# A hybrid decoder trunk on one core: gate and up of 2048 FFN columns by seven products of halves

## The chip, the cores and the metric

The kernel runs on one core of one Trainium2 chip. The metric is the device time of one execution in microseconds (us); of several runs the median is given. The profile is one execution recorded by the hardware profiler.

## What is computed

Two layers over 256 tokens of width 1024, in fp32. Layer 0 mixes tokens by gated linear attention, layer 1 by causal softmax attention with partial rotary positions. Each mixer and each feed-forward layer (FFN) is followed by a residual and a layer norm. The change touches the FFN alone:

```python
FFN_HIDDEN = 2816
def swiglu_ffn(x, w_gu, w_down):                     # x (256, 1024), w_gu (1024, 5632), w_down (2816, 1024)
    gate, up = jnp.split(x @ w_gu, 2, axis=-1)
    return (jax.nn.silu(gate) * up) @ w_down
# x <- LN(alpha*x + mixer(x));  x <- LN(alpha*x + swiglu_ffn(x))
```

## The kernel before

Every operation is entered in a plan (`Plan.op`) with its engine, an estimated length, and the tiles it reads and writes. `emit()` then places each engine's operations in time by these lengths, greedily: what can start first goes first, among equals the one that stands earlier in the program, with some operations marked urgent. The resulting order on each engine is fixed; at run time each engine works through its own list and waits by semaphores. Buffers of 4 KB per partition (kind S, 38 slots) are handed out in program order: a new buffer is given out only when enough slots stay free for all earlier buffers that have none yet. So loads, which stand on SP's queue, run ahead of their use as far as the slots allow. PSUM has four banks of kind acc, which hold the sums of the down product for the whole FFN, and four of kind ps.

Weights are fp32. A unit of 512 KB (128 partitions x 1024) is loaded by SP and split by `split`: ACT copies it into a rounded high part (L258), DVE subtracts that from the raw unit to give the low part (L259). `w_kcols` takes slices of the contraction, `w_row` one row block of the down weights. A product is three matmuls (`mm3`, L286 to L288): high by high, low by high, high by low. The activations are kept transposed and split as well (tiles xT, kind T); `transpose_split` makes them by four 128x128 transposes on PE into one PSUM bank (L301), a copy on ACT (L310) and a subtraction on DVE (L314).

In `ffn` the first 512 of the 2816 columns are computed with tokens in rows: stationary xT, moving weights of 512 columns (banks pg and pu, `act_block`), silu on ACT (L439), the product on DVE (L440), then `transpose_split` into hT0. The other 2304 columns are nine rounds of 256 columns with features in rows: stationary weights of 128 columns, moving xT of both token halves, 256 wide (bank gu), so that silu (L480), product (L482) and split (L485, L487) leave hT already in the layout that the down product needs. Each round needs four units (g and u, two slices each). A row block of 128 of these columns is then multiplied by its row of the down weights (`down`, banks fy, 512 wide, both token halves); the list `pend` delays it by a round, and the last three rounds' (six row blocks) come at the end, one half of the output at a time, each token half followed by its `layer_norm`. In the layer norm GpSimd (POOL) takes a power of one column (L354); POOL has next to nothing else to do in the FFN.

Of the kernel before, what the change touches and what calls it, by code (L numbers as in the profile page):

```python
# [11 lines left out]
AF = mybir.ActivationFunctionType  # L12
# [4 lines left out]
P = 128  # L17
# [17 lines left out]
SLOTS = 38  # L35
# [5 lines left out]
class Buf:  # L41
    """A tile of the plan: gets a slot of its kind when its first writer is placed."""
# [147 lines left out]
def kernel(ctx, tc, x, positions, gla_w_in, gla_w_gk, gla_b_gk, gla_norm_g, gla_w_out,  # L190
# [104 lines left out]
    def transpose_split(src, dst, t, half, skey=None, dstf=None, dkey=None, n=4):  # L295
# [38 lines left out]
    def layer_norm(xo, y, gb, dstT, t, last=False):  # L334
# [21 lines left out]
        for hf in range(2):  # L356
# [13 lines left out]
            else:  # L370
                transpose_split(xn, dstT, t, hf, skey=hf)
        return xn

# [37 lines left out]
    def out_proj(aT, w, xo, gb, dstT):  # L411
        ws = [w_row(f"wo{k}", w, k) for k in range(KT)]
        xn = []
        for t in range(2):
# [8 lines left out]
            xn.append(layer_norm(xo[t], y, gb, dstT, t))  # L423
        return xn

# [1 line left out]
    def ffn(i, xs, T, gb, dstT, last):  # L427
# [31 lines left out]
        NB = (HID - 512) // 256  # L459
        for b in range(NB):  # L460
# [297 lines left out]
    xs = out_proj(ogT, gla_w_out[0], xs, gb, T1)  # L758

# [41 lines left out]
    xs = ffn(0, xs, T1, gb, T2, False)  # L801

# [113 lines left out]
    xs = out_proj(oT, moba_w_out[0], xs, gb, T3)  # L916
    gb = load_ln(1, 1)
    ffn(1, xs, T3, gb, None, True)
# [39 lines left out]
```

## Time and profile before

| | us |
|---|---|
| median of 3 runs | 608.55 (606.66 to 609.45) |
| span of the profiled execution | 605.5 |
| PE busy | 592.4 (98%) |
| DVE busy | 385.4 (64%) |
| ACT busy | 282.7 (47%) |
| POOL busy | 23.4 (4%) |
| DMA queue q1, share of 16 engines | 55.4% |

The profiled execution has no time beside its span; the runs' median lies 3.05 us above it. In the 40 slices PE is at 9 tenths in all but the first and the last. Matmul durations of single rows overlap, since matmuls are pipelined; the distance from one start to the next is what one costs.

### The profile page before, as it was taken

Reading aid. Unit: us, or ns where it says so; the run is one execution under the profiler, and the core shown is the slowest. Engines: PE = TensorE matmul, PEld = TensorE weight load, DVE = VectorE, ACT = ScalarE, POOL = GpSimd, SP = SyncE. Lnnn points to the kernel's source line nnn. Section 1 sums busy time; section 2 is a strip of 40 time slices with the busy share of each in tenths; the row PEclk is TensorE's granted clock in tenths of the full one; section 3 lists DMA queues with packets and bytes.
Section 4 is the critical chain, followed back from the end, with each engine's and each line's share of the span. In section 5 each row is a group of like instructions: output and inputs, shape, how many; then the busy total and the mean of one; then the engine's idle time right before and its main releaser. Section 6 shows DMA issues by size and latency. Waiting matters only on the chain.

```text
span 605.5 us, 9405 instructions
## 1 busy us (share of the span) xinstructions
PE 592.4 (98%) x3806; PEld 538.3 (89%) x3806; DVE 385.4 (64%) x523; ACT 282.7 (47%) x396; POOL 23.4 (4%) x27
## 2 busy tenths in 40 slices
PE   7999999999999999999999999999999999999995
PEld 6899887888899999999889999888899999999983
DVE  5897269986554555454695788999665554555226
ACT  4892365355444344444363456637454444444110
POOL 1020211100000000000000000000000000000001
PEclk9999999999999999999999999999999999999998
DMA  8974194667655556545375455536765665665001
GB/s 280 381 223 159 63 296 159 211 203 227 195 186 190 178 175 209 178 171 175 104 244 180 146 164 193 188 110 239 246 207 176 207 197 186 193 184 180 2 2 69
DMA packets 68270, 110.13 MB, mean 182 GB/s; under 512 B 4689, under 2 KB 42097, under 8 KB 68226
## 3 DMA queue, kind: packets, MB, share of 16 engines
q1 hardware_dynamic: 68226, 109.53, 55.4%
q8 instruction: 30, 0.49, 0.3%
q14 instruction: 14, 0.11, 0.1%
HBM read 108.47 MB, written 1.05 MB: 181 GB/s over the span
## 4 chain that ended last, share of the span: by engine, by line
PE 94%; DMA 3%; DVE 1%; ACT 0%; issue 0%; POOL 0%; SPq 0%; DVEq 0%; ACTq 0%
PE gu L286 11%; PE gu L288 11%; PE gu L287 11%; PE fy L286 7%; PE fy L288 7%; PE fy L287 7%; PE v L288 2%; PE v L286 2%; PE v L287 2%; PE y L286 2%; PE y L288 2%; PE y L287 2%; PE tr L301 1%; PE mq L286 1%; PE mk L288 1%; PE mk L286 1%
## 5 line engine op out<-in xcount | busy, mean ns | idle before, releaser
L482 DVE TENSOR_TENSOR sil<-gu,sil 128x256 f32<-128x256 f32 x36 | 15.3, 424 | 53.0 <-ACT sil L480 53.0
L480 ACT ACTIVATE sil<-gu 128x256 f32<-128x256 f32 x36 | 13.8, 384 | 63.9 <-PE gu L288 63.9
L354 POOL TENSOR_TENSOR st<-st,mhalf 128x1 f32<-128x1 f32 x8 | 7.6, 944 | 496.8 <-DVE st L352 496.8
L487 DVE TENSOR_TENSOR hT<-sil,hT 128x256 fp32r<-128x256 f32 x36 | 15.2, 424 | 13.7 <-ACT hT L485 13.7
L485 ACT CAST hT<-sil 128x256 fp32r<-128x256 f32 x36 | 14.6, 406 | 17.3 <-DVE sil L482 17.3
L310 ACT CAST xT<-tr 128x512 fp32r<-128x512 f32 x16 | 8.7, 588 | 22.4 <-PE tr L301 22.4
L314 DVE TENSOR_TENSOR xT<-tr,xT 128x512 fp32r<-128x512 f32 x16 | 10.4, 685 | 5.7 <-ACT xT L310 5.6
L342 DVE SCALAR_TENSOR_TENSOR r<-xn,fy 128x512 f32<-128x512 f32 x8 | 5.5, 684 | 11.3 <-PE fy L288 11.3
L346 DVE BATCH_NORM_STATS2 st<-r 128x6 f32<-128x512 f32 x16 | 11.1, 694 | 0.5
L364 DVE SCALAR_TENSOR_TENSOR xn<-r,st,lnb 128x512 f32<-128x512 f32 x16 | 11.3, 744 | 0.0
L360 DVE SCALAR_TENSOR_TENSOR r<-r,st,lng 128x512 f32<-128x512 f32 x16 | 11.2, 744 | 0.0
L734 DVE SCALAR_TENSOR_TENSOR og<-o,ss,sg 128x256 f32<-128x256 f32 x8 | 3.5, 476 | 5.9 <-POOL sg L695 5.9
L695 POOL TENSOR_TENSOR sg<-sg,normg 128x512 f32<-128x512 f32 x4 | 6.4, 1594 | 15.1 <-ACT sg L691 15.1
L866 ACT ACTIVATE pr<-ms,mst 128x128 f32<-128x128 f32 (+1 forms) x16 | 6.6, 422 | 0.6 <-DVE mst L861 0.6
L301 PEld LDWEIGHTS tr<-ident,xn 128*128 128x128 f32 x48 | 5.6, 141 | 0.8
L301 PE MATMUL tr<-ident,xn 128*128 128x128 f32 x48 | 6.2, 272 | 0.0
L310 ACT CAST hT0h<-tr 128x512 fp32r<-128x512 f32 x4 | 2.3, 585 | 7.1 <-PE tr L301 7.1
L691 ACT ACTIVATE sg<-g 128x512 f32<-128x512 f32 x4 | 2.4, 594 | 6.9 <-PE g L288 6.8
L517 PE MATMUL junk<-zeros 128*128 128x128 f32 x22 | 4.4, 375 | 1.1 <-DVE zeros L510 1.1
L834 DVE TENSOR_TENSOR sw<-sw,rope 32x512 f32<-32x512 f32 x8 | 5.4, 672 | 0.0
L751 DVE TENSOR_TENSOR ogT<-trg,ogT 128x512 fp32r<-128x512 f32 x4 | 2.7, 682 | 4.1 <-ACT ogT L747 4.1
L259 DVE TENSOR_TENSOR u10l<-u10r,u10h 128x1024 fp32r<-128x1024 f32 x2 | 2.5, 1226 | 4.5 <-ACT u10h L258 4.5
(1207 smaller groups left out, 2439.0 us busy)
## 6 DMA issues: line engine op xcount, KB each, us to landing
lng<-in_ln_g SPq DMA_DIRECT2D x4, 512.0 KB, 4.0
lnb<-in_ln_b SPq DMA_DIRECT2D x4, 512.0 KB, 6.3
x<-in_x SPq DMA_DIRECT2D x4, 256.0 KB, 4.2
g00r<-in_ffn_w_gu SPq DMA_DIRECT2D x2, 512.0 KB, 3.5
g01r<-in_ffn_w_gu SPq DMA_DIRECT2D x2, 512.0 KB, 4.5
u00r<-in_ffn_w_gu SPq DMA_DIRECT2D x2, 512.0 KB, 7.0
u01r<-in_ffn_w_gu SPq DMA_DIRECT2D x2, 512.0 KB, 8.1
d0r<-in_ffn_w_down SPq DMA_DIRECT2D x2, 512.0 KB, 7.4
```

The source lines that it names most:

```text
L286: nc.tensor.matmul(ps, lh, rh, start=start, stop=False)
L287: nc.tensor.matmul(ps, ll, rh, start=False, stop=False)
L288: nc.tensor.matmul(ps, lh, rl, start=False, stop=stop)
L301: nc.tensor.transpose(ps.f[:, j * P:(j + 1) * P], src.f[:, k * P:(k + 1) * P], ident.f)
L310: nc.scalar.copy(view(0), ps.f.rearrange("p (k c) -> p k c", k=4))
L346: nc.vector.bn_stats(st.f[:, 6 * hf:6 * hf + 6], r.f[:, sl])
L360: nc.vector.scalar_tensor_tensor(out=r.f[:, sl], in0=r.f[:, sl], scalar=st.f[:, 12:13], in1=g.f[:, sl], op0=ALU.subtract, op1=ALU.mult)
L364: nc.vector.scalar_tensor_tensor(out=xn.f[:, sl], in0=r.f[:, sl], scalar=st.f[:, 15:16], in1=b.f[:, sl], op0=ALU.mult, op1=ALU.add)
L480: act(256, lambda ps=ps, sil=sil: nc.scalar.activation(sil.f[:, 0:S], ps.f[:, 0:S], AF.Silu), [ps], [(sil, 0)], table="silu")
L482: dve(256, lambda ps=ps, sil=sil: nc.vector.tensor_tensor(out=sil.f[:, S:2 * S], in0=ps.f[:, S:2 * S], in1=sil.f[:, 0:S], op=ALU.mult), [p ...
L485: act(256, lambda c=c, sil=sil, hT=hT: nc.scalar.copy(hv(hT)[:, c, :], sil.f[:, S:2 * S]), [(sil, 1)], [(hT, c)])
L487: dve(256, lambda c=c, sil=sil, hT=hT: nc.vector.tensor_tensor(out=hv(hT)[:, 2 + c, :], in0=sil.f[:, S:2 * S], in1=hv(hT)[:, c, :].bitcast ...
```

## The change

For four blocks of 512 columns (the columns 512 to 2559) of each layer, gate and up are computed together as a product of 2x2 block matrices: the left matrix has the two token halves as rows and the two halves of the contraction as columns, the right one the two halves of the contraction as rows and gate and up as columns. Seven products of halves, with sums of x on the left and sums of weights on the right, take the place of eight. Tokens stand in rows: stationary parts of x, moving weights of 512 columns.

The sums of x (s1 to s4) are made once a layer by `x_sums` from an unsplit copy of the transposed x, which `transpose_split` now keeps (`keep`, an added ACT copy), and are split like everything else. The sums of weights are made in place: a unit is loaded by SP and split for its product, and then an accumulating DMA on POOL's queue (`dma_add`) adds the next quarter of the weights into the same buffer, which is split again. The chain `ch` goes through four products (a00, s1, s2, a11) with three such adds; `r4` goes through two (s4, s3) with one; `r3` is used once (a01). All seven products collect in three PSUM banks (pa, pc, pb), evicted in between by `keep_`. The results stand with tokens in rows, so each token half is transposed and split once a block. The down products of the block before are placed between the products (`down_now`). The last 256 columns stay as they were, and SLOTS is 41.

```diff
-SLOTS = 38
+SLOTS = 41
...
+    def dma_add(fn, reads, writes, **kw):
+        return pl.op("POOL", 1.3, fn, reads, writes, extra=4.0, **kw)
...
@@ transpose_split
             act(512, hi, [ps], [(dst, ("h",) + kh)], urgent=True)
             dve(512, lo, [ps, (dst, ("h",) + kh)], [(dst, ("l",) + kh)], urgent=True)
+            if keep is not None:
+                act(512, lambda: nc.scalar.copy(keep[t].f[:, 512 * half:512 * half + 512], ps.f), [ps],
+                    [(keep[t], half)], urgent=True)
...
+    def x_sums(x32):
...
+        s13, s24 = S_("s13"), S_("s24")
+        out_ = {}
+        parts = (("s1", s13, 0, lambda: half(1, 0), lambda: half(1, 1), ALU.subtract, [(x32[1], 0), (x32[1], 1)]),
+                 ("s2", s24, 0, lambda: s13.f[:, 0:512], lambda: half(0, 0), ALU.subtract, [(s13, 0), (x32[0], 0)]),
+                 ("s3", s13, 1, lambda: half(0, 0), lambda: half(1, 0), ALU.subtract, [(x32[0], 0), (x32[1], 0)]),
+                 ("s4", s24, 1, lambda: half(0, 1), lambda: s24.f[:, 0:512], ALU.add, [(x32[0], 1), (s24, 0)]))
+        for n, b, j, a0, a1, op, reads in parts:
...
+            dve(512, lambda b=b, sl=sl, a0=a0, a1=a1, op=op: nc.vector.tensor_tensor(
+                out=b.f[:, sl], in0=a0(), in1=a1(), op=op), reads, [(b, j)])
+            hl = S_(n + "hl", True)
+            act(512, lambda b=b, sl=sl, hl=hl: nc.scalar.copy(hl.r[:, 0:512], b.f[:, sl]), [(b, j)], [(hl, 0)])
+            dve(512, lambda b=b, sl=sl, hl=hl: nc.vector.tensor_tensor(
+                out=hl.r[:, 512:1024], in0=b.f[:, sl], in1=hl.f[:, 0:512], op=ALU.subtract), [(b, j), (hl, 0)],
+                [(hl, 1)])
...
+        def unit(kh, gu, q, c0):
+            k0 = 4 * kh + 2 * q
+            return wgu[k0 * P:(k0 + 2) * P, HID * gu + c0:HID * gu + c0 + 512].rearrange("(k p) c -> p k c", p=P)
...
+        def split_unit(name, raw):
+            hi, lo = S_(name + "h", True), S_(name + "l", True)
+            act(1024, lambda: nc.scalar.copy(hi.r, raw.f), [raw], [hi])
+            dve(1024, lambda: nc.vector.tensor_tensor(out=lo.r, in0=raw.f, in1=hi.f, op=ALU.subtract), [raw, hi], [lo])
+            return hi, lo
...
+        def seven(b, c0, pend):
+            pa, pc, pb = pl.buf("ps", "pa"), pl.buf("ps", "pc"), pl.buf("ps", "pb")
+            e1, e2 = S_("e1"), S_("e2")
...
+            def product(ps, left, ws, first, last_):
+                st, rd = lhs(left)
+                for q, (wh, wl) in enumerate(ws):
+                    def f(q=q, wh=wh, wl=wl):
+                        for j in range(2):
+                            sh, sl_ = st(2 * q + j)
+                            cs = slice(512 * j, 512 * j + 512)
...
+                    pe(6 * 512, f, rd + [wh, wl], [ps])
...
+            def add_to(raws, kh, gu):
+                for q in range(2):
+                    def f(q=q):
+                        nc.gpsimd.dma_start(uv(raws[q]), unit(kh, gu, q, c0), accum_op=ALU.add)
+                    dma_add(f, [raws[q]], [raws[q]])
+
+            ch = [load_unit(f"A{q}", unit(0, 0, q, c0)) for q in range(2)]
+            product(pa, "a00", [split_unit(f"A{q}", ch[q]) for q in range(2)], True, False)
+            keep_(pa, e1, 0)
+            add_to(ch, 0, 1)
+            product(pc, "s1", [split_unit(f"B{q}", ch[q]) for q in range(2)], True, False)
+            keep_(pc, e2, 0)
+            r3 = [load_unit(f"C{q}", unit(1, 0, q, c0)) for q in range(2)]
+            product(pb, "a01", [split_unit(f"C{q}", r3[q]) for q in range(2)], True, True)
...
+            add_to(ch, 1, 1)
+            product(pa, "s2", [split_unit(f"D{q}", ch[q]) for q in range(2)], False, False)
+            keep_(pa, e1, 1)
+            r4 = [load_unit(f"E{q}", unit(1, 1, q, c0)) for q in range(2)]
+            down_now(pend[:2])
+            product(pc, "s4", [split_unit(f"E{q}", r4[q]) for q in range(2)], False, True)
...
+            transpose_split(e1, (h, l), 0, 0, skey=0, dkey=0, dstf=lambda i: dst(i, slice(0, P)))
+            add_to(r4, 0, 1)
+            product(pa, "s3", [split_unit(f"F{q}", r4[q]) for q in range(2)], False, False)
...
+            down_now(pend[2:])
+            add_to(ch, 1, 0)
+            product(pa, "a11", [split_unit(f"G{q}", ch[q]) for q in range(2)], False, True)
...
+            transpose_split(e2, (h, l), 1, 1, skey=1, dkey=1, dstf=lambda i: dst(i, slice(P, 2 * P)))
...
-        NB = (HID - 512) // 256
-        for b in range(NB):
+        for b in range(4):
+            pend = seven(b, 512 + 512 * b, pend)
+        for b in (8,):
             c0 = 512 + 256 * b
...
-            if b < NB - 2:
-                for k, bufs, f in pend:
-                    ws = w_row(f"d{k}", wd, k)
-                    for t in range(2):
-                        down(k, t, bufs, f, ws)
-                pend = []
```

## Rows read from the trace of the kernel before

**Rows 1.** The page, parts 1 and 2: busy time, and tenths in 40 slices
```profile
PE 592.4 (98%) x3806; PEld 538.3 (89%) x3806; DVE 385.4 (64%) x523; ACT 282.7 (47%) x396; POOL 23.4 (4%) x27
...
PEclk9999999999999999999999999999999999999998
DMA  8974194667655556545375455536765665665001
```

**Rows 2.** The page, part 4: the chain that ended last, share by engine
```profile
PE 94%; DMA 3%; DVE 1%; ACT 0%; issue 0%; POOL 0%; SPq 0%; DVEq 0%; ACTq 0%
```

**Rows 3.** Busy time by stretch: length, each engine's busy us, clock, DMA share, GB/s
```profile
core 0: us, PE busy (x) PEld busy (x) DVE busy (x) ACT busy (x) POOL busy (x), PEclk, DMA share, GB/s
...
90.00:120.00 30.00, 28.81 (x133) 23.11 (x132) 27.91 (x51) 13.54 (x17) 3.36 (x3) 1.00 0.56 184
120.00:150.00 30.00, 28.67 (x164) 24.97 (x163) 22.13 (x24) 15.93 (x19) 0.71 (x1) 1.00 0.67 221
...
201.00:218.00 17.00, 17.00 (x123) 16.04 (x122) 8.96 (x10) 6.82 (x10) 0.00 (x0) 1.00 0.57 186
```

**Rows 4.** The chain in order of time, 411 to 424: start us, us held, what
```profile
411.94 0.24 PE pg L286
...
417.31 0.23 PE pg L288
417.55 0.87 PE tr L301 x8
```

**Rows 5.** PE in order of time, 185 to 196: start, duration, operation (pipelined)
```profile
184.88 0.28 PE L288 MATMUL gu<-xT,u20h 128*128 128x256 f32 x1
...
193.64 0.40 PE L286 MATMUL fy<-d6h,hT 128*128 128x512 f32 x1
...
195.93 0.39 PE L287 MATMUL fy<-d6h,hT 128*128 128x512 f32 x1
```

**Rows 6.** One unit of the fifth round: ns min/median/max, first and last start
```profile
L256 SPq DMA_DIRECT2D g50r<-in_ffn_w_gu x2: 378/378/379, 193.8 to 486.5; - x2
L258 ACT CAST g50h<-g50r x2: 1051/1052/1052, 197.8 to 491.4; 128x1024 fp32r<-128x1024 f32 x2
L259 DVE TENSOR_TENSOR g50l<-g50r,g50h x2: 1226/1226/1226, 198.9 to 492.5; 128x1024 fp32r<-128x1024 f32 x2
...
DMA to landing us min/median/max: 3.9/4.4/4.8
...
L286 PE MATMUL gu<-xT,g50h x16: 277/281/283, 233.1 to 529.2; 128*128 128x256 f32 x16
```

**Rows 7.** Lines L439, L440, L310 and L314: ns min/median/max, first and last start
```profile
L439 ACT ACTIVATE sil<-pg x4: 584/597/611, 125.6 to 430.1; 128x512 f32<-128x512 f32 x4
...
L440 DVE TENSOR_TENSOR sil<-pu,sil x4: 680/683/683, 129.8 to 435.8; 128x512 f32<-128x512 f32 x4
...
L310 ACT CAST xT<-tr x16: 576/588/594, 5.1 to 418.5; 128x512 fp32r<-128x512 f32 x16
...
L314 DVE TENSOR_TENSOR xT<-tr,xT x16: 679/683/692, 5.7 to 419.3; 128x512 fp32r<-128x512 f32 x16
```

**Rows 8.** DMA of the stretch 15 to 30: packets, rate, share of 16 engines
```profile
DMA packets 3398, 5.71 MB, mean 381 GB/s; under 512 B 360, under 2 KB 744, under 8 KB 3397
...
q1 hardware_dynamic: 3397, 5.70, 105.4%
```

**Rows 9.** DMA issues of the stretch 105 to 125: KB each, us to landing
```profile
fu02r<-in_ffn_w_gu SPq DMA_DIRECT2D x1, 512.0 KB, 3.4
...
u01r<-in_ffn_w_gu SPq DMA_DIRECT2D x1, 512.0 KB, 8.1
```

**Rows 10.** The first unit behind the opening 512 columns: issue and first use
```profile
L256 SPq DMA_DIRECT2D g00r<-in_ffn_w_gu x2: 367/368/368, 113.6 to 407.2; - x2
...
L286 PE MATMUL gu<-xT,g00h x16: 277/282/365, 140.8 to 439.8; 128*128 128x256 f32 x16
```

**Rows 11.** Waits of SP's queue: us in total, times, longest
```profile
SPq L256 <- PE gu L288: 62.8, 23, 5.4
```

**Rows 12.** The page, part 5: POOL's part of the layer norm
```profile
L354 POOL TENSOR_TENSOR st<-st,mhalf 128x1 f32<-128x1 f32 x8 | 7.6, 944 | 496.8 <-DVE st L352 496.8
```

More of the change, by code (lines that the diff above doesn't have):

```diff
@@ L293, in new_T, with transpose_split @@
         return b
-    def transpose_split(src, dst, t, half, skey=None, dstf=None, dkey=None, n=4):
+    def transpose_split(src, dst, t, half, skey=None, dstf=None, dkey=None, n=4, keep=None):
         ps = pl.buf("ps", "tr")
@@ L332, in load_ln, with layer_norm @@
         return g, b
-    def layer_norm(xo, y, gb, dstT, t, last=False):
+    def layer_norm(xo, y, gb, dstT, t, last=False, keep=None):
         g, b = gb
@@ L370, in layer_norm @@
             else:
-                transpose_split(xn, dstT, t, hf, skey=hf)
+                transpose_split(xn, dstT, t, hf, skey=hf, keep=keep)
         return xn
@@ L422, in out_proj, with half, ffn @@
                 pe(3 * 512, f, aT.keys(t, k) + list(ws[k]), [y[hf]])
-            xn.append(layer_norm(xo[t], y, gb, dstT, t))
+            xn.append(layer_norm(xo[t], y, gb, dstT, t, keep=keep))
         return xn
-    def ffn(i, xs, T, gb, dstT, last):
+    def x_sums(x32):
+        def half(t, kh):
+            return x32[t].f[:, 512 * kh:512 * kh + 512]
+        s13, s24 = S_("s13"), S_("s24")
[5 more added lines that the diff above has]
+        for n, b, j, a0, a1, op, reads in parts:
+            sl = slice(512 * j, 512 * j + 512)
+            dve(512, lambda b=b, sl=sl, a0=a0, a1=a1, op=op: nc.vector.tensor_tensor(
[5 more added lines that the diff above has]
+                [(hl, 1)])
+            out_[n] = hl
+        return out_
+    def ffn(i, xs, T, gb, dstT, last, x32):
         wgu, wd = ffn_w_gu[i], ffn_w_down[i]
@@ new lines, in down_now, with keep_, dst @@
+        def down_now(items):
+            for k, bufs, f in items:
+                ws = w_row(f"d{k}", wd, k)
+                for t in range(2):
+                    down(k, t, bufs, f, ws)
+        def seven(b, c0, pend):
[8 more added lines that the diff above has]
+                            cs = slice(512 * j, 512 * j + 512)
+                            nc.tensor.matmul(ps.f, sh, wh.r[:, cs], start=first and q == 0 and j == 0, stop=False,
+                                             skip_group_check=True)
+                            nc.tensor.matmul(ps.f, sl_, wh.r[:, cs], start=False, stop=False, skip_group_check=True)
+                            nc.tensor.matmul(ps.f, sh, wl.r[:, cs], start=False, stop=last_ and q == 1 and j == 1,
+                                             skip_group_check=True)
+                    pe(6 * 512, f, rd + [wh, wl], [ps])
+            def keep_(ps, dst, j):
+                sl = slice(512 * j, 512 * j + 512)
+                act(512, lambda: nc.scalar.copy(dst.f[:, sl], ps.f), [ps], [(dst, j)])
+            def add_to(raws, kh, gu):
[11 more added lines that the diff above has]
+            product(pb, "a01", [split_unit(f"C{q}", r3[q]) for q in range(2)], True, True)
+            dve(512, lambda: nc.vector.tensor_tensor(out=e1.f[:, 0:512], in0=pb.f, in1=e1.f[:, 0:512], op=ALU.add),
+                [pb, (e1, 0)], [(e1, 0)])
+            act(512, lambda: nc.scalar.activation(e1.f[:, 0:512], e1.f[:, 0:512], AF.Silu), [(e1, 0)], [(e1, 0)],
+                table="silu")
+            add_to(ch, 1, 1)
[4 more added lines that the diff above has]
+            product(pc, "s4", [split_unit(f"E{q}", r4[q]) for q in range(2)], False, True)
+            h, l = S_(f"hT{b}h", True), S_(f"hT{b}l", True)
+            def dst(i, cs):
+                return (h, l)[i].r.rearrange("p (k c) -> p k c", k=4)[:, :, cs]
+            dve(512, lambda: nc.vector.tensor_tensor(out=e1.f[:, 512:1024], in0=pc.f, in1=e1.f[:, 512:1024],
+                                                     op=ALU.subtract), [pc, (e1, 1)], [(e1, 1)])
+            dve(512, lambda: nc.vector.tensor_tensor(out=e1.f[:, 0:512], in0=e1.f[:, 0:512], in1=e1.f[:, 512:1024],
+                                                     op=ALU.mult), [(e1, 0), (e1, 1)], [(e1, 0)])
+            transpose_split(e1, (h, l), 0, 0, skey=0, dkey=0, dstf=lambda i: dst(i, slice(0, P)))
+            add_to(r4, 0, 1)
+            product(pa, "s3", [split_unit(f"F{q}", r4[q]) for q in range(2)], False, False)
+            dve(512, lambda: nc.vector.tensor_tensor(out=e2.f[:, 0:512], in0=e2.f[:, 0:512], in1=pa.f,
+                                                     op=ALU.subtract), [pa, (e2, 0)], [(e2, 0)])
+            down_now(pend[2:])
+            add_to(ch, 1, 0)
+            product(pa, "a11", [split_unit(f"G{q}", ch[q]) for q in range(2)], False, True)
+            act(512, lambda: nc.scalar.activation(e2.f[:, 512:1024], pa.f, AF.Silu), [pa], [(e2, 1)], table="silu")
+            dve(512, lambda: nc.vector.tensor_tensor(out=e2.f[:, 512:1024], in0=e2.f[:, 512:1024], in1=e2.f[:, 0:512],
+                                                     op=ALU.mult), [(e2, 0), (e2, 1)], [(e2, 1)])
+            transpose_split(e2, (h, l), 1, 1, skey=1, dkey=1, dstf=lambda i: dst(i, slice(P, 2 * P)))
+            return [(c0 // P + j, (h, l), lambda j=j: (hv(h)[:, j, :], hv(l)[:, j, :])) for j in range(4)]
@@ L757 @@
     T1 = new_xT("xT1")
[L758 removed]
+    x32 = [S_("x32a"), S_("x32b")]
+    xs = out_proj(ogT, gla_w_out[0], xs, gb, T1, x32)
     posb, ang, kk_, rr_ = S_("posb"), S_("ang"), S_("kk"), S_("rr")
```

23 lines of the change are left out of this document (19 added, 4 removed).

## The prediction

> **What bounds the kernel now.** I read the page's busy shares first, then the chain that ended last, then a table of stretches, and only then single instructions. TensorE (PE) is busy 98% of the span at a granted clock of 9 tenths or more in every slice but the last [rows 1], and 94% of the chain is PE, DMA 3% [rows 2]. In the steady part of a feed-forward layer PE is busy 17.00 of 17.00 us, VectorE (DVE) 8.96, ScalarE (ACT) 6.82, the 16 DMA engines 0.57 of the time [rows 3]. So in that part a product removed from PE is time gained, as long as DVE, ACT and DMA still keep ahead. They are far ahead now: g50r is issued at 193.8 and g50h is first used at 233.1, 39 us later [rows 6]. What holds the loads back is buffers: SP's longest waits are for PE to be done with old ones [rows 11].
>
> **PE: what the change removes and adds.** For 512 FFN columns the kernel before runs two of its 256-column rounds: 2 x 96 = 192 matmuls with 256 moving columns. Such matmuls start every 0.120 us (73 steps from 184.88 to 193.64) [rows 5], so 23.04 us. The change runs 7 products x 4 slices of the contraction x 3 parts = 84 matmuls with 512 moving columns and x stationary. That form stands in the trace as pg: 24 from 411.94 to 417.55, 0.2337 us each [rows 4], so 19.6 us. New are two rounds of four transposes; eight of them hold the chain 0.87 us [rows 4]. Net 19.6 + 0.87 - 23.04 = -2.57 us for 512 columns; four such blocks in each of two layers give **-20.6 us**. The 48 down matmuls of a block stay: they start every 0.229 us (10 steps from 193.64 to 195.93) [rows 5], 11.0 us. So a block of 512 columns took 23.04 + 11.0 = 34.0 us (twice the 17 us of [rows 3]) and would take 31.5 us if PE never waits; four blocks: 136.1 before, 126.0 after.
>
> **DVE and ACT.** A weight unit (512 KB) is split by one ACT copy, 1.05 us, and one DVE subtraction, 1.23 us [rows 6]. Seven products need 14 units for gate and up where eight were loaded; with four down rows a block has 18 splits, not 12. DVE: 18 x 1.226 + five 512-wide operations at 0.683 + two transposed low parts at 0.683 [rows 7] = 26.9 us of 31.5 (before: 17.9 of 34.0). ACT: 18 x 1.05 + three evictions at 0.588 + two silu at 0.597 + two high parts at 0.588 = 23.0 us. Both fit, at 85% and 73%, so I cost them at nothing; without that cover each us of DVE per block would be 8 us. The four sums of x (eight 512-wide DVE operations, 5.5 us, and four ACT copies) and the eight extra ACT copies of the unsplit x come where DVE is busy 27.91 of 30 us and then 22.13 of 30 us [rows 3]. PE does not need them before the second product, some 25 us after the layer norm; but they push the first splits back. I take 0.2 us in all (bounds 0 and 5.5 us a layer, if the first sum were on the path).
>
> **DMA: the open term.** Before, a block loads 8 units of gate and up and 4 of down. After, it loads 6 + 4 and adds 8 more into buffers that are already there, from POOL's queue; the trace shows no add. A load at full pressure costs 524288 B / 381 GB/s = 1.38 us of all 16 engines [rows 8]. An add cannot cost less than a load, since as many bytes come from HBM and are written. It must also read what lies in the buffer, so the other end is two loads, 2.75 us. The sum per block is then 10 x 1.38 + 8 x 1.38 = 24.8 us, or 10 x 1.38 + 8 x 2.75 = 35.8 us, against 31.5 us of PE. Between these I take two loads: the row shows the engines bound by the packets that pass through them (their queue at 105% of the stretch), and an add passes twice the bytes on the reading side. So DMA becomes the tighter resource by 4.3 us a block.
>
> The Trainium skill speaks against this change here: Collectives: The Full Stack, section "The bandwidth ceiling: the fold count and why AG ≠ RS ≠ AR", has a reduce at half the rate of a copy, because two sources are read on one ring. By that an add would cost about two loads, the dear end; no run here shows it yet.
>
> **What softens it** is the lead. g00r, the first unit behind the opening 512 columns, is issued at 113.6 and first used at 140.8 [rows 10]. In those 27 us the first Strassen block can go from load to its fourth product's weights: load 4.4 [rows 6], three splits at 2.5 (1.05 + 1.23 + two hand-overs), two adds, and 2.5 for the second unit behind the first. With an add landing like a quick load, 3.4, that is 21.2 us; like the slowest of these loads, 8.1 [rows 9], 30.6 us. So about four loads and four adds, 5.5 + 11.0 = 16.5 us of DMA, are done when PE arrives. Four blocks then need 4 x 35.8 - 16.5 = 126.7 us at full use, 0.7 us over PE's 126.0 in each layer. Full use is not to be had: an add waits for the split of what landed before it, and at the head of the layer, where loads are most pressed, the share is only 0.67 [rows 3]. I take 97%: 4 x 36.9 - 16.5 = 131.1, a loss of **5.1 us a layer, 10.2 us in all**. Behind the Strassen blocks come a 256-column round and the last down products with weights that are loaded plainly; nothing is late there.
>
> **Queues that the adds pass.** An add stands on POOL and waits for ACT and DVE to have read the buffer. Behind it on POOL wait the other adds and, at the head of a layer, the layer norm's power -0.5 (L354, 0.94 us each, eight in all) [rows 12]; both are placed by the planner's times, and I cost that at 0 (bound: one late add, 8.1 us, once a layer). Behind an add that is late, ACT's and DVE's splits wait in order, and then PE: that is the stall counted above. A block's chain from load to fourth product must also fit in a period, because the next block's first buffer comes free only about when this block's fourth product is through (50 buffers a block, some 33 free): 21.2 to 30.6 us against 31.5 us fits, barely at the dear end.
>
> **The sum.** The profiled execution has a span of 605.5 us; the median of the runs, 608.55, lies 3.05 us above, which I keep as what lies around the span. 605.5 + 3.05 - 20.6 + 10.2 + 0.2 = 598.3, say **598 us**.
>
> **Rivals.**
> 1. *The adds are hidden altogether.* If an add costs at most (31.5 - 13.8) / 8 = 2.21 us, DMA stays under PE and the whole 20.6 us remain: 588 us. For it: 27 to 39 us of lead, DMA at 0.57 now. Against it: an add has two sources.
> 2. *Slower than before: DMA cannot be kept busy because each add hangs on a split.* Place: the waits of ACT's split for the second, fourth, sixth and seventh products. At two loads an add and 88% use a block takes 40.7 us; 4 x 40.7 - 16.5 = 146.3, 20.3 us over PE in each layer: 588 + 40.6 = 629 us. It decides from 38.1 us a block on ((136.1 + 16.5) / 4), that is below 94% use. For it: three splits and two adds in series in each period, beside loads that share the engines and stretch a landing from 3.4 to 8.1 us. Against it: PE that stalls stops freeing buffers, loads pause, and the adds get the engines.
> 3. *The gain is given back just about whole:* 95% use, 37.7 us a block, 134.2 a layer, 605 us.
> 4. *An add costs three loads* (read, read, write as separate passages, 4.13 us): 13.8 + 33.0 = 46.8 us a block, some 660 us. Nothing in the trace asks for it.
>
> **Chances.** Forecast, 592 to 605: 0.32. Rival 1, 587 to 592: 0.25. Rival 3, 605 to 612: 0.12. Rival 2, over 612: 0.27. Rival 4: 0.04. This kernel's runs can tell about 0.5%, 3 us, from no change: faster 0.57, same 0.12, slower 0.31. The range that should hold the time 8 times in 10 is 587 to 628; the likeliest case's own is 592 to 605.
>
> **What would show it.** PE: 84 matmuls of 128x512 per block at 0.233 us, and a block period of about 32.5 us; 31.5 means rival 1, over 38 rival 2. DMA: the share in the Strassen stretch near 9 tenths, and an add's time from issue to landing; landings near 4 us without load would speak for a cheap add. DVE near 85% there. If PE waits, the waits should name DVE low parts of the added units (second, fourth, sixth and seventh products), with ACT waiting for POOL's DMAs before them. The forecast is wrong if PE's waits name DVE with no DMA behind it, if POOL's issues themselves take several us each, or if PEclk falls in the stretch.

## The result, and the profile of the changed kernel

| | before | changed |
|---|---|---|
| median, us | 608.27 (606.66 to 609.45, 4 runs) | 663.84 (659.46 to 665.83, 4 runs) |
| profiled execution, us: span | 605.5 | 657.6 |
| its own time, us | - | 659.46 |

The changed kernel is slower: ratio 1.092, 95% interval 1.089 to 1.095, +55.6 us. The forecast was 598, its range 587 to 628.

The page of the changed kernel, parts 1 and 2 (answering rows 1), part 3 (queue: packets, MB, share of 16 engines) and part 4 (answering rows 2):

```profile
PE 594.4 (90%) x3006; PEld 500.3 (76%) x3006; DVE 457.9 (70%) x579; ACT 339.1 (52%) x452; POOL 100.0 (15%) x91
...
PEclk9999999998997998899999999999989979799998
DMA  8963572699999898997356446348999989999301
...
q1 hardware_dynamic: 47490, 101.14, 45.6%
q0 software_dynamic: 17408, 33.56, 29.3%
...
PE 45%; DMA 28%; issue 13%; DVE 8%; ACT 3%; POOL 1%; SPq 0%; DVEq 0%; POOLq 0%; ACTq 0%
```

PE issues 800 matmuls fewer (3006 against 3806) and is yet busy 594.4 us, 2.0 more than before; its clock drops in slices of the seven-product blocks (named Strassen blocks below); the DMA engines there are mostly at 8 or 9 tenths where they were mostly at 5 or 6; and DMA holds 28% of the chain where it held 3%. Three blocks of 512 columns, each from its first product to the next block's (columns as in rows 3):

```profile
142.00:177.40 35.40, 32.34 (x140) 26.32 (x139) 25.19 (x25) 20.83 (x24) 9.44 (x8) 0.95 1.07 275
177.40:220.00 42.60, 34.53 (x141) 27.59 (x140) 25.81 (x26) 22.94 (x27) 8.70 (x8) 0.92 0.97 227
220.00:260.00 40.00, 33.58 (x140) 26.61 (x139) 24.14 (x24) 19.76 (x24) 9.66 (x8) 0.91 0.96 230
```

A block was to take 31.5 us of PE and about 32.5 in all; the six periods from block to block inside the two layers are 35.8, 42.8, 40.4 and 37.0, 42.7, 41.4 us, 40.0 on average. What PE waited for (us in all, times, longest), and how long the DMAs of the page's part 6 took from issue to landing (KB, median us; rows 6 and 9 had 4.4 for a unit, 3.4 to 8.1 at the head of the layer):

```profile
PE tr L304 <- DVE e L577: 20.7, 7, 4.8
PE pa L536 <- ACT e L545: 19.0, 6, 4.1
PE tr L304 <- DVE e L588: 6.6, 4, 2.7
```
```profile
A<-in_ffn_w_gu POOLq DMA_DIRECT2D x48, 512.0 KB, 8.9
A<-in_ffn_w_gu SPq DMA_DIRECT2D x16, 512.0 KB, 8.4
...
E<-in_ffn_w_gu POOLq DMA_DIRECT2D x16, 512.0 KB, 9.8
```

The waits name ACT's eviction `e` and DVE's operations on `e`, not splits. These are short operations that stand in fixed lists behind splits, and the splits wait for adds. ACT's list between 201 and 245 us shows it (start, us, engine, line, operation, and in brackets the idle time before it with what ended it):

```profile
201.21 1.04 ACT L513 CAST G1h<-A 128x1024 fp32r<-128x1024 f32 x1 [1.32 <-DMA A<-in_ffn_w_gu]
...
202.64 1.05 ACT L513 CAST A0h<-A 128x1024 fp32r<-128x1024 f32 x1
...
205.48 1.04 ACT L513 CAST C1h<-C 128x1024 fp32r<-128x1024 f32 x1
213.50 1.05 ACT L513 CAST B0h<-A 128x1024 fp32r<-128x1024 f32 x1 [6.97 <-DMA A<-in_ffn_w_gu]
...
222.28 1.04 ACT L513 CAST D0h<-A 128x1024 fp32r<-128x1024 f32 x1
...
240.41 1.05 ACT L513 CAST G0h<-A 128x1024 fp32r<-128x1024 f32 x1 [2.92 <-DMA A<-in_ffn_w_gu]
...
244.69 1.05 ACT L513 CAST A0h<-A 128x1024 fp32r<-128x1024 f32 x1
```

Read it as one buffer's life: A0 split at 202.6, its first add landed in time for B0 at 213.5, the second for D0 at 222.3, the third for G0 at 240.4. Only behind G0 and G1 stands A0 of the next block, at 244.7: 42.05 us after the A0 of this one. Each block's chain of load, split, add, split, add, split, add, split begins when the chain before it is over. While ACT stands 6.97 us at B0, the transposed part and the evictions behind it in the list stand too. It is the list that holds A0 here, not its buffer: these two A units were issued at 186.0 and 189.5, at the end of the second and the start of the fourth product of the block before, and had landed by 198.5.

A stall of PE can cost a second time. PE's timeline behind a wait of 4.09 us, and the table of that stretch:

```profile
244.84 0.80 PE L536 MATMUL pa<-F0h,s3hl 128*128 128x512 f32 x1 [4.09 <-ACT e L545]
245.43 0.63 PE L538 MATMUL pa<-F0h,s3hl 128*128 128x512 f32 x1
245.86 0.63 PE L539 MATMUL pa<-F0l,s3hl 128*128 128x512 f32 x1
...
249.27 0.63 PE L538 MATMUL pa<-F1h,s3hl 128*128 128x512 f32 x1
249.70 0.63 PE L539 MATMUL pa<-F1l,s3hl 128*128 128x512 f32 x1
```
```profile
245.00:250.00 5.00, 5.00 (x12) 3.64 (x12) 4.80 (x5) 3.57 (x4) 2.44 (x2) 0.50 0.94 306
```

From start to start these matmuls take 0.427 us (nine steps from 245.86 to 249.70), not 0.234: the granted clock is 0.50, the lower of its two levels (1.2 and 2.4 GHz). Of the 14 waits of 1.9 to 4.8 us that PE has within the blocks, 11 have matmuls at this pace behind them; those of 2.71 us before 184.2, 3.30 before 522.3 and 3.19 before 614.4 have none.

### The profile page after: what moved, and what is told of

Read it like the earlier page. It is cut to its first block, busy times and chain, and to the rows that moved or that the text cites. A ratio compares the mean times of both kernels' runs of the same rounds, so it can differ in the third digit from the quotient of the medians.

```text
span 657.6 us, 8111 instructions
## 1 busy us (share of the span) xinstructions
PE 594.4 (90%) x3006; PEld 500.3 (76%) x3006; DVE 457.9 (70%) x579; ACT 339.1 (52%) x452; POOL 100.0 (15%) x91
## 3 DMA queue, kind: packets, MB, share of 16 engines
q1 hardware_dynamic: 47490, 101.14, 45.6%
q0 software_dynamic: 17408, 33.56, 29.3%
HBM read 133.63 MB, written 1.05 MB: 205 GB/s over the span
## 4 chain that ended last, share of the span: by engine, by line
PE 45%; DMA 28%; issue 13%; DVE 8%; ACT 3%; POOL 1%; SPq 0%; DVEq 0%; POOLq 0%; ACTq 0%
DMA A<-in_ffn_w_gu 20%; PE fy L289 3%; PE fy L290 3%; PE fy L291 2%; PE v L291 2%; PE v L289 2%; PE v L290 2%; DMA g81r<-in_ffn_w_gu 2%; PE y L291 2%; PE y L289 2%; PE y L290 2%; DMA d5r<-in_ffn_w_down 2%; PE tr L304 2%; DMA C<-in_ffn_w_gu 1%; DMA E<-in_ffn_w_gu 1%
## 5 line engine op out<-in xcount | busy, mean ns | idle before, releaser
L550 POOL DMA_DIRECT2D A<-in_ffn_w_gu x48 | 58.3, 1237 | 200.9 <-DVE A0l L514 85.5
L304 PE MATMUL tr<-ident,e 128*128 128x128 f32 x64 | 11.2, 303 | 27.4 <-DVE e L577 20.7
L304 PEld LDWEIGHTS tr<-ident,e 128*128 128x128 f32 x64 | 7.7, 151 | 32.7 <-issue 32.5
L514 DVE TENSOR_TENSOR B0l<-A,B0h 128x1024 fp32r<-128x1024 f32 x8 | 9.8, 1223 | 20.8 <-ACT B0h L513 20.8
L550 POOL DMA_DIRECT2D E<-in_ffn_w_gu x16 | 19.4, 1214 | 22.1 <-DVE E0l L514 12.0
L514 DVE TENSOR_TENSOR G0l<-A,G0h 128x1024 fp32r<-128x1024 f32 x8 | 9.8, 1223 | 13.4 <-ACT G0h L513 13.4
L514 DVE TENSOR_TENSOR B1l<-A,B1h 128x1024 fp32r<-128x1024 f32 x8 | 9.8, 1225 | 13.3 <-ACT B1h L513 13.3
L514 DVE TENSOR_TENSOR G1l<-A,G1h 128x1024 fp32r<-128x1024 f32 x8 | 9.8, 1224 | 13.0 <-ACT G1h L513 13.0
L514 DVE TENSOR_TENSOR F0l<-E,F0h 128x1024 fp32r<-128x1024 f32 x8 | 9.8, 1224 | 12.4 <-ACT F0h L513 12.4
L513 ACT CAST G0h<-A 128x1024 fp32r<-128x1024 f32 x8 | 8.4, 1053 | 16.1 <-DMA A<-in_ffn_w_gu 16.1
L514 DVE TENSOR_TENSOR F1l<-E,F1h 128x1024 fp32r<-128x1024 f32 x8 | 9.8, 1225 | 9.5 <-ACT F1h L513 9.5
L514 DVE TENSOR_TENSOR D1l<-A,D1h 128x1024 fp32r<-128x1024 f32 x8 | 9.8, 1225 | 7.8 <-ACT D1h L513 7.8
```

Source lines behind the costliest of these rows:

```text
L513: act(1024, lambda: nc.scalar.copy(hi.r, raw.f), [raw], [hi])
L514: dve(1024, lambda: nc.vector.tensor_tensor(out=lo.r, in0=raw.f, in1=hi.f, op=ALU.subtract), [raw, hi], [lo])
L550: nc.gpsimd.dma_start(uv(raws[q]), unit(kh, gu, q, c0), accum_op=ALU.add)
```

## The experiments

Two theories ran through all runs; the expectations call them T1 and T2, or Theory 1 and Theory 2. T1: the adds take too much time of the 16 DMA engines. T2: an add lands too late in a chain of split and add, within lists whose order is fixed. T3 (or Theory 3) and T4, below, are about what the planner was told of an add: T3 that it placed the adds' landing too early, T4 that it did not know that adds take the engines from the loads. First what a run gives by a simple measure: "links" is the mean time from the end of DVE's low part to the start of ACT's next copy of the same buffer, for A to B, B to D and D to G, over eight blocks and both halves; "period" the mean of the six distances between first products of successive blocks. Both are taken from the traces' starts and ends.

| kernel | median, us | links A-B + B-D + D-G, us | period | period less links |
|---|---|---|---|---|
| changed | 663.8 | 9.1 + 7.7 + 12.6 = 29.4 | 40.0 | 10.6 |
| e1_plain | 596.6 | 6.3 + 7.0 + 7.8 = 21.1 | 32.2 | 11.1 |
| e15_plain_39 | 594.5 | 6.5 + 6.7 + 7.6 = 20.8 | 31.9 | 11.1 |
| e12_plain_twice | 635.8 | 7.5 + 7.3 + 10.8 = 25.6 | 37.1 | 11.5 |
| e14_scratch_first | 634.5 | 7.3 + 7.3 + 10.4 = 25.0 | 36.1 | 11.1 |
| e2_thin_down | 630.9 | 8.0 + 7.2 + 10.1 = 25.3 | 37.3 | 12.0 |
| e13_plain_late | 751.5 | 11.5 + 8.2 + 16.1 = 35.8 | 51.7 | 15.9 |
| e3_planned | 631.6 | 12.3 + 11.7 + 12.1 = 36.1 | 34.6 | -1.5 |
| e16_overlap | 642.4 | 10.9 + 9.1 + 18.6 = 38.6 | 38.7 | 0.1 |

### The adds as plain loads

```diff
- nc.gpsimd.dma_start(uv(raws[q]), unit(kh, gu, q, c0), accum_op=ALU.add)
+ nc.gpsimd.dma_start(uv(raws[q]), unit(kh, gu, q, c0))
```

> The 64 adds become plain loads of the same bytes into the same buffers, still issued by POOL, with the same waits and the same order on every engine; the sums of weights are left out, so the second, fourth, sixth and seventh products have wrong weights. Theory 1 (the DMA engines are full: in the trace of after an add holds the 16 engines 29.3% x 657.6 us / 64 = 3.0 us, a load 1.5 us, so a block asks for 10 x 1.5 + 8 x 3.0 = 39 us): 18 x 1.5 = 27 us a block, under PE's 31.5, so 588 to 598 us. Theory 2 (what is dear is POOL's way of issuing, or the chain of splits and transfers in series): the landing stays near 9 us and the time over 640 us.

596.56 us, ratio 0.984 (0.982 to 0.986). Same operations, same order, same bytes from HBM; only that nothing is accumulated. Its page:

```profile
PE 574.6 (97%) x3006; PEld 489.3 (82%) x3006; DVE 456.0 (77%) x579; ACT 340.2 (57%) x452; POOL 69.0 (12%) x91
...
DMA  8984285248889899897366446526788788879101
...
q0 software_dynamic: 9216, 33.56, 16.7%
...
A<-in_ffn_w_gu POOLq DMA_DIRECT2D x48, 512.0 KB, 6.0
```

So without the accumulation PE is busy 17.8 us less than before the change and the kernel is 10 us faster (596.56 against 606.28 for the kernel before beside it), as T1 had it; 67 us hang on the accumulation alone. Queue q0 carries just the 64 adds: 29.3% of 657.6 us / 64 = 3.01 us of 16 engines for an add, against 16.7% of 594.7 / 64 = 1.55 us for a plain load of the same piece, 1.94 times as much. SP's loads in the changed kernel come to 45.6% of 657.6 / 193 units of 512 KB = 1.55 us as well. In the changed kernel there is a stretch, 150.9 to 156.0, in which the engines carry nothing but adds and a single other packet (the DMA view: packets and rate, then the queues' share of 16 engines; answering rows 8, where they carried nothing but loads at 381 GB/s):

```profile
DMA packets 540, 1.04 MB, mean 204 GB/s; under 512 B 32, under 2 KB 32, under 8 KB 540
...
q0 software_dynamic: 539, 1.04, 112.4%
q1 hardware_dynamic: 1, 0.00, 0.1%
```

Full engines move 204 GB/s of adds: 524288 B / 204 GB/s = 2.57 us, at 112% of the engines 2.89 us of their time.

The Trainium skill's rule that the prediction cited (Collectives: The Full Stack, section "The bandwidth ceiling: the fold count and why AG ≠ RS ≠ AR": a reduce goes at half the rate of a copy) is stated there for collectives in a ring; for a transfer from HBM into a buffer the runs here show nearly the same factor, 1.94.

> e1_plain (adds as plain loads, weight sums left out) with SLOTS 39 in place of 41, the same lead as e12_plain_twice has. If the 39 us between e1_plain and e12_plain_twice are the second load's time on the engines, this stays within 1% of e1_plain: 594 to 603 us. If they are the two slots, it comes near 620 to 636 us.

594.52 us, ratio 0.981 (0.978 to 0.985): two slots fewer cost nothing. This kernel (SLOTS 39 for 41 in e1_plain) is the base for the next ones.

### The engines' time without late landing, and late landing without the engines' time

A second plain load per add, into a scratch buffer that nobody reads; in e14_scratch_first it is issued ahead of the first:

```diff
  nc.gpsimd.dma_start(uv(raws[q]), unit(kh, gu, q, c0))
+ nc.gpsimd.dma_start(uv(sc), unit(1 - kh, 1 - gu, q, c0))
```

> The weight sums are left out: each add is a plain load of the same quarter into the same buffer (as in e1_plain), and behind each of them POOL issues a second plain load of another quarter into a scratch buffer that nobody reads (SLOTS 39 for the room). So the 16 engines move per block 10 + 8 + 8 = 26 loads of 1.55 us = 40 us, about what the changed kernel asks of them (39.5), but the buffer that the next split waits for is filled by a plain load, not by an add. Theory T1 (the engines' time is what costs): close to the changed kernel, 635 to 665 us, DMA share 0.95 or more in the blocks. Theory T2 (what costs is how long an add takes from issue to landing, in series between splits in fixed lists): A and E land as in e1_plain, 6 to 7 us, and the time stays near e1_plain, 596 to 612 us.

635.76 us, ratio 1.050 (1.046 to 1.054), at the low end of what T1 gave. Two blocks:

```profile
177.30:214.80 37.50, 33.41 (x142) 26.54 (x141) 25.52 (x26) 22.49 (x27) 11.56 (x16) 0.95 0.99 366
214.80:252.10 37.30, 34.25 (x142) 27.21 (x141) 25.63 (x26) 21.46 (x26) 11.55 (x16) 0.91 0.98 366
```

The engines are full (0.99 and 0.98), with no add among the DMAs: so 41 of the 69 us between e15_plain_39 and the changed kernel appear in this order with full engines alone, the longer links that come with them (25.6 against 20.8) included. The other 28 come with the adds themselves, and two causes stand side by side there: their links are 3.8 us a block longer (29.4 against 25.6; eight blocks, 30 us), and they ask 1.9 us a block more of the engines (39.6 against 37.7, both worked out below; eight blocks, 15 us).

> As e12_plain_twice (the weight sums left out, a second plain load into scratch beside each plain load that stands for an add, SLOTS 39), but POOL issues the scratch load first. The engines move the same bytes with the same instructions; only what the next split waits for lands later, by the issue of one load and its time on the engines, some 2 to 3 us (A some 9 us after the split releases POOL where e12_plain_twice has some 7). T2 (landing in series in fixed lists counts by itself): three links a block, 2 to 3 us each, as far as they are not hidden: 645 to 670 us against 635.8. T1 (the engines' time alone): within 1% of e12_plain_twice, 630 to 642 us.

634.49 us, ratio 1.046 (1.043 to 1.050). The edit did not do what was meant: the links are 25.0 us, no longer than in e12_plain_twice, so it repeats that run within 0.2%, as T1 had it, and tells nothing on T2.

Now the other side: plain loads, and behind each pair POOL issues for each buffer a load of 2 KB into it, which waits for the first.

```diff
+ pl.op("POOL", 0.65, lambda q=q: nc.gpsimd.dma_start(uv(raws[q])[:, 0, 0:4], unit(kh, gu, q, c0)[:, 0, 0:4]),
+       [raws[q]], [raws[q]], extra=2.7)
```

> The weight sums are left out as in e1_plain; each add is a plain load, and after the two of a pair POOL issues for each buffer a load of 4 columns (2 KB) into the same buffer, which has to wait for the first to land. The planner is told the same 4 us behind the issue as for an add. So the 16 engines move 18 loads a block, 28 us, as in e1_plain, but what the next split waits for comes some 3 to 4 us later, 9 to 10 us behind the first issue, as an add does in the changed kernel. Theory T2 (late landing in series in fixed lists): the changed kernel's stalls come back, 630 to 660 us, PE waiting for tr behind DVE e and for pa, with the DMA share at 0.8 or less. Theory T1 (the engines' time): near e1_plain, 596 to 610 us.

751.46 us, ratio 1.239 (1.234 to 1.243), above even T2's range. Two blocks:

```profile
194.90:243.60 48.70, 36.55 (x141) 29.21 (x140) 23.39 (x25) 20.14 (x24) 8.84 (x14) 0.82 0.56 185
243.60:293.70 50.10, 36.46 (x142) 28.89 (x142) 25.77 (x26) 21.62 (x26) 10.13 (x16) 0.86 0.56 189
```

With the engines at 0.56, as idle as before the change (rows 3), the blocks take 50 us: long links cost PE its time without full engines. But this is not late landing alone, and the size is not to be carried over: POOL's waits for the first loads (207 us at A, 63 at E) hold up the loads behind them, and PE falls to clocks of 0.82 and 0.86. That an add's own landing would be enough is not shown.

### Which of the two sets the period

In six kernels the period is the links plus 11 us (10.6 to 12.0), while the links range from 21 to 29 us: the three splits between them, the next A's split and the hand-overs make up the rest. This shows that in these lists one chain follows on the other, not that the chain is what makes the period: in e1_plain and e15_plain_39, whose blocks take hardly more than the 31.5 us that PE needs, the sum is the same. The next kernel tests it; it lets two chains overlap at unchanged bytes:

```diff
             add_to(r4, 0, 1, c0)
+            early = ahead(nxt) if nxt else None      # load, split and first add of the next block's A
```

> The changed kernel, sums and all, but the load, the split and the first add of the next block's A stand in the program ahead of this block's third add and its last product, so that ACT's list has A of the next block ahead of F and G of this one; in the changed kernel it has them behind G, so each block's chain of A, B, D, G starts only when the one before has ended, and the period is the three links from split to split (29.4 us on average) and 11 us. The planner still takes 4 us for an add. Theory T2 with that place (chains end to end set the period): the period falls by about the first link, to 33 to 37 us, and the time to 615 to 642 us. Theory T1 (the engines' 39.5 us a block set the period): 652 to 668 us as in the changed kernel.

642.42 us, ratio 1.057 (1.052 to 1.061), just above T2's range for the time and far below T1's. In ACT's list A of the next block now stands ahead of F and G of this one:

```profile
186.92 1.05 ACT L513 CAST A0h<-A 128x1024 fp32r<-128x1024 f32 x1 [0.30 <-DMA A<-in_ffn_w_gu]
192.15 1.05 ACT L513 CAST A1h<-A 128x1024 fp32r<-128x1024 f32 x1 [4.17 <-DMA A<-in_ffn_w_gu]
...
195.92 1.05 ACT L513 CAST F0h<-E 128x1024 fp32r<-128x1024 f32 x1 [2.23 <-DMA E<-in_ffn_w_gu]
...
198.35 1.04 ACT L513 CAST G0h<-A 128x1024 fp32r<-128x1024 f32 x1
```

The links are 9 us longer than in the changed kernel, and the period is 1.4 us shorter, 38.7 us, where T2 had 33 to 37; the last block of a layer is shorter too, 37.7 and 37.8 us from its first product to the end of its last, where it was 43.3 and 39.9. So the end-to-end chain was a bound, and 21 us are had by lifting it. What is left is close to the engines' time (10 loads at 1.55 + 8 adds at 3.01 = 39.6 us a block), and from 182.2 to 257.0 the engines' share is 1.05 and 1.02.

The planner gets there too, if it is told a longer landing:

```diff
- return pl.op("POOL", 1.3, fn, reads, writes, extra=4.0, **kw)
+ return pl.op("POOL", 1.3, fn, reads, writes, extra=7.6, **kw)
```

> The planner is told that an add lands 7.6 us after its issue, not 4.0 (after: 8.9 to 9.8 us); everything else is that of after, only the order of the operations can differ. Theory 1 (full DMA engines): no order makes the engines faster, the time stays within 2% of after's 664 us. Theory 3 (an order planned with adds that land too early puts operations at the head of ACT's, DVE's and PE's lists that must wait for an add): 20 us or more less.

631.62 us, ratio 1.042 (1.039 to 1.045): the order alone is worth 32 us, where T1 had less than 2%. ACT's list again has A0 of the next block ahead of F0, and both A units ahead of G; the periods are 32.8, 37.2, 33.7 and 32.5, 36.2, 35.2, but the fourth block of each layer takes 42.0 and 41.3 us from its first product to its last.

The engines' time lowered instead: the down rows loaded at an eighth of their bytes.

```diff
- dma(lambda: nc.sync.dma_start(raw.f, w[k * P:(k + 1) * P, :]), 512, [], [raw])
+ dma(lambda: nc.sync.dma_start(raw.f[:, 0:128], w[k * P:(k + 1) * P, 0:128]), 512, [], [raw])
```

> The down weights that are used between the Strassen blocks are loaded as 128 columns, an eighth of the bytes, and the split repeats these columns over 1024, so ACT, DVE, PE and the order of all queues are those of after; only DMA has less to do (the down product of these rows is wrong). The adds and their chain stay whole. Theory 1 (full DMA engines): 3.5 loads x 1.5 us less in each of 8 blocks, about 42 us less: 615 to 630 us, and the adds land earlier. Theory 2 (the chain of splits and adds in series sets the period): under 12 us less, over 650 us.

630.88 us, ratio 1.041 (1.037 to 1.045). A block:

```profile
176.80:215.30 38.50, 32.85 (x142) 26.53 (x141) 27.44 (x28) 23.02 (x28) 9.86 (x9) 0.96 0.86 190
```

The time is 33 us less, at the upper end of what T1 had (42 less, 615 to 630) and far from T2's (over 650). In the block shown the engines have room (0.86) and PE waits all the same; in the other three of the layer their share is 0.99, 0.96 and 0.94. The links are 4 us a block shorter (25.3 against 29.4), so less work for the engines and a shorter chain come together here. With both edits:

> e3_planned (all eight Strassen blocks, landing planned at 7.6 us) with the down weights between the blocks loaded as 128 columns and repeated by the split, as in e2_thin_down (the down product of these rows is wrong). If after's loss is made up of full DMA engines and of the order together, both are mended here: 590 to 604 us. If something else stretches a block (the chain in series, the clock), over 612 us.

621.13 us, ratio 1.023 (1.016 to 1.031), where 590 to 604 was expected: each edit gives about 32 us, both together 43. The first periods are 30.8, 32.6 and 31.1, 31.2 us, as PE wants them; the third and fourth of each layer 37 to 40 (the fourth to the start of its last product).

### Fewer blocks

Two of the four blocks of a layer go back to rounds of 256 columns (7 for a block, r for a round):

```diff
-        for b in range(4):
-            pend = seven(b, 512 + 512 * b, pend)
+        order = '7rr7rrr'
```

> Two Strassen blocks in each layer, not four, each followed by two 256-column rounds of before (the last two rounds as in before); the result is whole. DMA by the prices of after: 2 x 39 + 5 rounds x 6 x 1.5 = 123 us a layer, PE 2 x 31.5 + 5 x 17 = 148 us. Theory 1: DMA has room again, half of the PE gain is had: 608.3 - 4 x 2.57 = 598 us, at most 604. Theories 2 and 3: each Strassen block still costs PE 5 to 10 us of waits: 610 to 635 us.

623.08 us, ratio 1.027 (1.025 to 1.029). Half the blocks should have left 598 to 604; they still lose some 25 us against 598, 6 us each. Over the layer the engines are at 7 to 9 tenths, but not in the blocks: the first of each layer takes 39.0 and 39.9 us with the engines at 0.96 and 0.94, the second 34.5 and 35.2 us at 0.87.

> e4_two with the landing of an add planned at 7.6 us after its issue instead of 4.0 (its adds landed after 7.6 to 9.8 us); the result is whole. Theory 3 (the order planned with too early landings put waiting operations at the head of the lists; that alone kept e4_two at 623 us): 597 to 605 us. Theory 1 alone (full DMA engines) has no room to act here, with 123 us of DMA for 148 us of PE in a layer; a time over 612 would need another cause, such as the length of the chain of splits and adds.

625.44 us, ratio 1.032 (1.026 to 1.038): what gave 32 us with four blocks in a row gives nothing here. T3 does not account for a block among rounds.

> Three Strassen blocks a layer, each followed by one 256-column round, with the landing planned at 7.6 us; the result is whole. DMA by the packet prices of after (load 1.34, add 2.83): 3 x 35.8 + 3 x 8 = 131 us, by the mean prices (1.5, 3.0) 3 x 39 + 3 x 9 = 144 us, PE 3 x 31.5 + 3 x 17 = 145 us. Theory 1 and 3 together: between 593 (608.3 - 6 x 2.57) and 605 us, faster than e5_two_planned if full use is reached, slower if not.

640.31 us, ratio 1.055 (1.049 to 1.061): far above the expected 593 to 605; three blocks a layer are worse than four with the same plan (631.6).

> e5_two_planned, and the evictions and combinations between the Strassen products (e1, e2) are marked urgent, so that they are not placed behind splits that are made ahead. The result is whole. Theory 3 in the narrower form, that PE's waits for e come from splits ahead of it in DVE's list: 2 to 6 us less than e5_two_planned. Otherwise the same within 0.5%.

628.00 us, ratio 1.033 (1.027 to 1.040): the evictions and combinations on `e` marked urgent give nothing (0.4% above e5_two_planned).

T4: the planner does not know that an add takes the engines from the loads. The next planner gives an add 2.9 us of SP's load line as well, and lets it land 2.3 us behind that:

```diff
+            if o.share:
+                clock["SP"] = max(clock["SP"], st) + o.share
+                o.end = max(st + o.dur, clock["SP"]) + o.extra
```

> e4_two with another planner: an add now also takes 2.9 us of the time line on which the planner places SP's loads (before, loads and adds were planned as if each had the DMA engines to itself), and lands 2.3 us after that. Only the order of the operations can differ; the result is whole. Theory 4 (fixed lists that were planned without the shared engines: a burst of adds makes loads made ahead land late, these stand at the head of ACT's and DVE's lists, and PE waits for e behind them): 597 to 608 us. If the order is not it, and the chain of splits and adds in series is: over 617 us, as e4_two and e5_two_planned.

625.09 us, ratio 1.030 (1.025 to 1.035): no gain. With four blocks:

> The kernel of after with the planner of e9_two_shared; the result is whole. Theory 4 with full DMA engines as the floor (36 to 39 us a block where PE needs 31.5): 610 to 630 us. If the order is not it: 631 us, as e3_planned, or more.

702.50 us, ratio 1.158 (1.155 to 1.162): 39 us worse than the changed kernel; PE waits 16.2 us for F1's copy and 10.9 for ACT's `e` in product `pa`. T4 falls as a remedy in both.

Last, the second block's A one round ahead, at the plan of e5_two_planned:

> e5_two_planned (two Strassen blocks a layer, among rounds of 256 columns, adds planned to land 7.6 us behind their issue), with the load, the split and the first add of the second block's A one round (17 us) earlier in the program. If the chain in series is what each block still costs (some 7 us each), the second block of each layer costs next to nothing more: 610 to 618 us against 625. If it is the engines' being full for a stretch around the adds, 620 to 630 us. To beat the kernel before (606) it would have to save the first blocks' share as well, which is not touched.

623.07 us, ratio 1.025 (1.020 to 1.030), 2 us less than e5_two_planned: not the 610 to 618 of the chain theory, but within the 620 to 630 of engines that are full for a stretch around the adds. The second block's A was split 47 us ahead of its first product in layer 0 (173.6 against 220.8), and the link from E to F is 15.5 us on average. No version with these adds beat the kernel before.

## Why the prediction was wrong

**PE: right.** In e15_plain_39 PE is busy 572.8 us, 19.6 less than before; predicted was 20.6, and the span is 591.6, 13.9 less. The periods of 31.9 us are the forecast's 31.5 and what little PE waits.

**DVE and ACT, the sums of x, POOL's issues: small, as costed.** All of them are in e15_plain_39 too, and its span falls 5.7 us less than PE's busy time (13.9 against 19.6), which leaves 5.7 us for all of these and for whatever else PE waits for.

**Behind the Strassen blocks: right.** From the start of the last product to the end of the last down matmul it takes 32.1 us in layer 0 and 31.1 in layer 1, both in the changed kernel and in e15_plain_39, though in the changed kernel the loads g80r to u81r land only after 12 to 15 us.

**The engines' time of an add: the right choice, every term short, 28 us.** Two loads an add is what was measured (1.94). But a load is 1.55 us, not 1.38: the row that gave 381 GB/s had the engines at 105% [rows 8], and 1.38 x 1.05 is 1.45; whence the rest was not tried. An add is 3.01 us, not 2.75; a block 39.6, not 35.8. By the forecast's own sum, with the lead at these prices too (4 x 1.55 + 4 x 3.01 = 18.2), 4 x 39.6 / 0.97 - 18.2 = 145.1 us a layer, 19.1 over PE: 588 + 38.2 + 0.2 = 626 us, 28 above the forecast and still within its range. So the prices alone do not explain 664; by this sum the other 38 us go to the step below, the clock's part included. e12_plain_twice, which comes close to this demand without adds (10 loads at 1.50 and 16 at 1.42 by its queues, 37.7 us a block), took 636.

**The step that failed** is the paragraph on the queues, and with it the 97% use in the sum. It cost the placing by the planner's times at 0, and it let a block's chain "from load to fourth product" with two adds, 21.2 to 30.6 us, fit in a period. What the runs showed in its place:

- The landing. An add landed after 8.9 and 9.8 us (medians), later than the dear end's 8.1, and the planner had placed it at 4.0. Telling it 7.6 changed the order alone and gave 32 us (e3_planned).
- The length. The chain is one add too short: the seventh product needs a third add. The three links take 29.4 us, and with the splits it is 40 us from block to block.
- The place. The next block's first buffer did come free early, even behind the second product; but in ACT's list its first split stands behind G's, so the chains run end to end. Where two may overlap, 21 us come back (e16_overlap).

In the sum's own terms: the four blocks take 162.4 and 161.0 us from the first product to the end of the last, where 131.1 a layer was forecast. At the measured prices that is a use of 0.88 (4 x 39.6 / 0.88 - 18.2 = 161.8); e3_planned, with 148.6 and 148.1 us, has 0.95.

**The rivals.** Rival 2 had the place (the splits that hang on adds) and its 88% use, but at its own price of an add, which gave 629. Its argument against itself, that a stalled PE gives the engines to the adds, does not help where adds hang on each other: e13_plain_late takes 50 us a block with the engines at 0.56. Rival 4's "some 660" is near the 664 by luck: an add took 1.94 loads and not three, and by the other rivals' sum its 46.8 us a block give 4 x 46.8 - 16.5 = 170.7 us a layer and 677.

**Left out altogether: PE's clock.** It was named only as what would make the forecast wrong. PE is busy 594.4 us in the changed kernel against 572.8 for the same instructions in e15_plain_39. So of the 66.0 us between the two spans (657.6 - 591.6), 21.6 are longer matmuls, at a mean granted clock of 0.963 against 0.996, and 44.4 are waits.

**What stays open.** Engines and chain are coupled, since a full engine makes links long; e12_plain_twice gives 41 us for the demand in this order, e16_overlap and e3_planned give 21 to 32 us back for another order, and these do not add up to one split. Nor is it shown why a block among rounds loses 6 us (e4_two, e5_two_planned, e8_two_urgent, e9_two_shared, e17_two_ahead). The link from E to F is late in four of these (17.9 us in e5_two_planned, 15.7 in e8_two_urgent, 12.6 in e9_two_shared, 15.5 in e17_two_ahead), but 10.2 in e4_two, as in the changed kernel (10.3); that the engines are full in the first block of a layer (0.96 and 0.94 in e4_two) is a rival that no run took away.

## What to carry to other kernels

An operand that is updated in place turns buffers that were loaded far ahead into a chain: count every link (landing, split, issue) up to the point where the buffer, or its place in a fixed list, is free for the next round, and compare that with the period, apart from the engines' busy time. When a landing is costed, take the one under the load that the change itself brings, and tell the planner the same; with four blocks in a row that gave 32 us here, with two among rounds nothing. And where PE may stall, count the matmuls behind the stall at the lower clock: here a third of the loss was that.

## What the runs showed of the hardware

An accumulating DMA of 512 KB took 3.01 us of the 16 DMA engines where the plain one took 1.55, and a stretch full of it moved 204 GB/s where one full of loads had moved 381 [rows 8]. On queue q0 an add was 272 packets and the plain load of the same piece 144 (17408 and 9216 packets for 64 each). POOL needed 1.2 us to issue it and 0.73 us for the plain one (part 5 of the pages of the changed kernel and of e1_plain: 58.3 us for 48 of them, and 35.0):

```profile
L550 POOL DMA_DIRECT2D A<-in_ffn_w_gu x48 | 58.3, 1237 | 200.9 <-DVE A0l L514 85.5
```
```profile
L550 POOL DMA_DIRECT2D A<-in_ffn_w_gu x48 | 35.0, 728 | 159.5 <-DVE A0l L514 59.3
```

It landed in 8.9 us (median) where the plain one landed in 6.0. And behind 11 of 14 waits of 1.9 to 4.8 us PE ran at the lower level for some us: 0.427 us a 512-column matmul, not 0.234, for 5 us behind a wait of 4.09.
